# A decoder layer on one core: ten gathered rows moved in front of the up-projection, and the small products of token mixing spread over four row groups

## The chip, the cores and the metric

The kernel runs on one core of a Trainium2 chip. The metric is the device time of one execution in microseconds (us). Engines are named as in the profile: PE (matrix products; PEld its weight loads), DVE (VectorE), ACT (ScalarE), POOL (GpSimd, which issues the indirect DMAs), SP (the queue that issues most other DMAs).

## What is computed

One decoder layer on 512 tokens of width 1024: token mixing (an mLSTM with four heads beside sliding-window attention), cross-attention into 256 memory tokens, and PEER, a layer of 128 x 128 single-neuron experts of which each token uses 8 heads x 16.

```python
h = h + concat([hm, ha]) @ w_out          # token mixing: mLSTM heads, attention heads
h = h + memory_cross_attention(rmsnorm(h, g_cross), rmsnorm(mem, g_mem), ...)
h = h + peer_ffn(rmsnorm(h, g_ffn), ...)
# peer_ffn: u = expert_down[eidx]; a = gelu(einsum("thkd,td->thk", u, x)); coef = g * a
#           out = einsum("thkd,thk->td", expert_up[eidx], coef)
return rmsnorm(h, g_final)
```

Inside the mLSTM the decay of one head is `d = exp(log_d - m_t)` with `log_d` the sum of a row that depends on the query, a column that depends on the key, and the causal mask.

## The kernel before, in words

The 512 tokens are four blocks of 128. Products in fp32 precision are made of three products of rounded parts (hi x hi, lo x hi, hi x lo); a product of plain fp32 operands is two passes on PE.

**Token mixing** (`front`). The input projection is done as GEMMs (`gemm_tm`, `gemm_fm`). For the mLSTM decays, `ra` is a tile of four partitions (one for each head) by 512 tokens. For each head, L218 multiplies it by a selector `sel` of four rows, which copies the head's row to all 128 partitions of the PSUM tile `ab`; L219 adds the causal mask `cmask`; ACT takes the exponential in four pieces (L222, tile `dt`). L230 makes the scores `st` of two heads from operands of 64 partitions each, L233 (DVE) multiplies scores and decays. L238 does for `wi` (two tiles `wb`) what L218 does for `ra`. PE fills the time between with the last input GEMM (`acc_f`, for `aq`). Then a list of letters, `MIX`, sets PE's order by hand: s is a step of window attention of a block (`sp` scores, `tp_p` transposes, `o_att`), m a step of the mLSTM, n the transposes `tp_hm` of its output, x a half of the output GEMM (`acc_o`), w the load of a weight.

**PEER** treats the blocks in two ways. Blocks 1 to 3 run over all 128 x 128 experts densely: for each of 128 "down tiles" (`Down`, 24 products `acc_d`) and 128 "up tiles" (`up_tile` and `up_mm`, 18 products `acc_u` of 512 columns). Their gates are scattered into the DRAM tensors `wd` by POOL (L672) or written there from `stg` by ACT's queue (L731), and read back as `wt` (L855). Block 0 is done sparsely by `gather`: 128 indirect DMAs fetch one row of `expert_down` per token each (L749, 128 x 1024 fp32), DVE takes the dot product of each with the token (L755, `dots`); then 128 more fetch rows of `expert_up`, and DVE adds each with its coefficient to `gacc` (L765). One call of `step(ga, 1)` does one row. Eight buffers `rows` hold the fetched rows, so a fetch waits for DVE to be done with the row eight before.

The rows of block 0 are laid out among the dense work: twelve in the last block of `gating` (at the steps in `GQ`), the other 244 in the loop over up tiles, by the weights `WST` and `WTL` and up to tile `GST` = 122 (the list `due`, L1165 to L1168). Between the two lie the `LEAD` = 7 down tiles that PE does before the first up tile. After the loop `finish` adds `gacc` and the PSUM sums to the residual `hb` (L907), normalises (L913) and writes out. A scheduler in the build then fixes each engine's order; on the chip each engine runs its list strictly in that order.

Of the kernel before, what the change touches and what calls it, by code (L numbers as in the profile page):

```python
# [48 lines left out]


GQ = range(9, 32, 2)
GST = 122
WST, WTL = 3, 5


# [2 lines left out]

MIX = ("w0 s0 s0 n0 n1 s1 m2 s1 x0 m2 s0 w1 x1 s0 m3 x0 s2 s1 s2 s1 s3 s1 s3 n2 x1 x2 s2 n3 s2 x3 s2 s3 x2 s3 s3 x3")


CROSS = "m0 o0 K1 K0 V0 V1 n0 q0 s0 s1 q1 s2 p0 s3 p1 p2 p3"
# [15 lines left out]
def front(c):  # L80
# [66 lines left out]
    A.activation(u, gf, AF.Abs)  # L147
    A.activation(u, u, AF.Exp, scale=-1.0)
    V.tensor_scalar(w1, u, 1.0, None, op0=ALU.add)
    ra = fp.tile([4, NB, P], F32, name="ra")  # L150
    raf = ra.rearrange("p b t -> p (b t)")
    V.scalar_tensor_tensor(raf, w1, -1.0, u, op0=ALU.add, op1=ALU.subtract)
    A.activation(w1, w1, AF.Ln)
    V.tensor_tensor(w1, w1, raf, op=ALU.subtract)
# [4 lines left out]
    V.memset(rs[:, :, 0:1], 0.0)  # L159
    V.tensor_tensor_scan(u, rs.rearrange("p b t -> p (b t)"), gf, 0.0, op0=ALU.mult, op1=ALU.add)  # L160
    V.tensor_tensor(raf, u, m, op=ALU.subtract)
    V.tensor_tensor(gi, gi, u, op=ALU.subtract)
    mp = fp.tile([4, NB], F32, name="mp")
    al = fp.tile([4, NB], F32, name="al")
# [3 lines left out]
    rows = f1.tile([P, S], F32, name="rows")  # L168
    V.memset(rows, 0.0)
    V.tensor_copy(rows[0:4], gi)  # L170
    wi = fp.tile([4, NB, P], F32, name="wi")
    for b in range(NB):
        t = slice(b * P, (b + 1) * P)
        A.activation(rows[32:36, t], gi[:, t], AF.Exp, bias=al[:, b:b + 1])
        A.activation(wi[:, b], ra[:, b], AF.Exp, bias=mp[:, b:b + 1])
    A.activation(rows[64:68], m, AF.Exp, scale=-1.0)
    cols = fp.tile([P, NB, 96], F32, name="cols")
    for b in range(NB):
        tp = ps.tile([P, 512], F32, tag="a", name="tp_r")
# [30 lines left out]
    gemm_tm(c, [a["w_in_m"][2, hf] for hf in range(2)], evac_mo)  # L210


    pt = []
    for pr in range(2):
        dts = []
        for h in (2 * pr, 2 * pr + 1):
            ab = ps.tile([P, 512], F32, tag="d", name="ab")
            T.matmul(ab, c.sel[:, h], raf, start=True, stop=False)  # L218
            T.matmul(ab, c.identb, c.cmask, start=False, stop=True)  # L219
            dt = c.np_.tile([P, D], F32, tag="xs", bufs=4, name="dt")[:, :S]  # L220
            for b in range(NB):
                A.activation(dt[:, b * P:(b + 1) * P], ab[:, b * P:(b + 1) * P], AF.Exp, bias=cols[:, b, h:h + 1])  # L222
            dts.append(dt)

        sts = [ps.tile([P, 512], F32, tag="a", name="st") for _ in range(2)]
        for b in range(NB):
            t = slice(b * P, (b + 1) * P)
            for hh in range(2):
                r = slice(64 * hh, 64 * hh + 64)
                T.matmul(sts[hh][:, t], qk[r, 2 + pr, t], qk[r, pr, t], start=True, stop=True)  # L230
        for hh in range(2):
            pth = fp.tile([P, S], F32, name=f"pt{2 * pr + hh}")
            V.tensor_tensor(pth, sts[hh], dts[hh], op=ALU.mult)  # L233
            pt.append(pth)
    dec = fp.tile([P, 2, NB], F32, name="dec")
    for pr in range(2):
        wb = ps.tile([P, 512], F32, tag="d", name="wb")
        T.matmul(wb, c.selp[:, pr], wi.rearrange("p b t -> p (b t)"), start=True, stop=True)  # L238
        V.tensor_copy(dec[:, pr], wb.rearrange("p (b t) -> p b t", b=NB)[:, :, P - 1])
        V.tensor_tensor(qk[:, pr], wb, qk[:, pr], op=ALU.mult)  # L240
    def make_kw(b):
# [818 lines left out]
def front_consts(c):  # L1060
    nc, a, cp = c.nc, c.a, c.fp
    V, G = nc.vector, nc.gpsimd
    c.gmh = cp.tile([P, 512], F32, name="gmh")
    c.sinks = cp.tile([P, 8], F32, name="sinks")
    with c.tc.issue_after(c.x_dma.ins):
        nc.sync.dma_start(c.gmh, a["prow"][0, 5120:5632].partition_broadcast(P))
        nc.sync.dma_start(c.sinks, a["prow"][0, 5632:5640].partition_broadcast(P))

    c.cmask = cp.tile([P, 512], BF16, name="cmask")
    z = c.np_.tile([P, D], F32, tag="xs", bufs=4, name="zmask")  # L1070
    V.memset(z[:, :512], 0.0)
    cm = c.np_.tile([P, D], F32, tag="xs", bufs=4, name="cm32")
    G.affine_select(cm[:, :512], z[:, :512], [[0, NB], [1, P]], ALU.is_ge, NEG, base=0, channel_multiplier=-1)
    V.tensor_copy(c.cmask, cm[:, :512])
    c.band = cp.tile([P, 256], F32, name="band")

    G.affine_select(c.band[:, 0:P], z[:, 0:P], [[1, P]], ALU.is_gt, NEG, base=0, channel_multiplier=-1)
    G.affine_select(c.band[:, P:256], z[:, 0:P], [[-1, P]], ALU.is_ge, NEG, base=0, channel_multiplier=1)

    c.sel = cp.tile([4, 4, P], F32, name="sel")  # L1080
    o = c.np_.tile([P, D], F32, tag="xs", bufs=4, name="ones4")[0:4, 0:512].rearrange("p (h q) -> p h q", h=4)
    V.memset(o, 1.0)
    G.affine_select(c.sel, o, [[1, 4], [0, P]], ALU.is_equal, 0.0, base=0, channel_multiplier=-1)
    c.selp = cp.tile([4, 2, P], F32, name="selp")
    G.affine_select(c.selp, o[:, 0:2], [[2, 2], [1, 2], [0, 64]], ALU.is_equal, 0.0, base=0, channel_multiplier=-1)


def body(tc, a, out, dbg=None):
# [3 lines left out]
    with ExitStack() as st:  # L1092
# [57 lines left out]
        with pool("gather", side="right") as c.gp:  # L1150
# [4 lines left out]
            c.up = st.enter_context(pool("up"))  # L1155
            assert len(gel) == SP

            ahead(LEAD)
            c.rowid = c.gp.tile([P, P], I32, name="rowid")
            with tc.issue_after(c.dl.ins):  # L1160
                nc.vector.tensor_copy(c.rowid, c.eidx)
            pst_ = [c.ps.tile([P, 512], F32, tag=t, name="acc_u") for t in "bbbbaa"]
            acc = [[pst_[2 * b], pst_[2 * b + 1]] for b in range(ND)]
            last, mms = [], []
            g0 = len(GQ)  # L1165
            due = [WST * u + WTL * made_by(u) for u in range(-1, GST)]
            rows = [(2 * P - g0) * (d - due[0]) // (due[-1] - due[0]) for d in due]
            rows += [rows[-1]] * (NK - GST)  # L1168
# [102 lines left out]
```

## Time and profile before

| | |
|---|---|
| median of 3 runs | 1662.37 us (1662.21 to 1662.63) |
| the profiled execution's own time | 1659.86 us |
| its span | 1658.1 us |
| PE / DVE / ACT / POOL busy, share of span | 97% / 74% / 44% / 36% |
| chain that ended last, by engine | PE 89%, DVE 5%, DMA 3%, ACT 2%, issue 1% |
| PE's granted clock over the span | 0.989 |

The profile is one execution. The profiled execution lies 2.5 us under the median, and its span 1.8 us under its own time. A view by windows gives the busy time of each engine in a stretch; a timeline gives the instructions in order with the idle time before each in square brackets and what ended it.

### The profile page before, as it was taken

To read this page: it belongs to the slowest core of one execution; us is meant where nothing else is said; L and a number is where in the kernel's file an instruction comes from. 1 tells how busy PE (TensorE), PEld (TensorE's weight loads), DVE (VectorE), ACT (ScalarE), POOL (GpSimd) and SP (SyncE) were. 2 spreads that over 40 slices of the span, in tenths; PEclk is the share of its full clock that TensorE was granted. 3 is DMA by queue.
4 is the path that set the end of the run, shared out by engine and by line. 5 is a ranking of instruction groups with operands and counts; after the bars stand their busy time and mean duration, and the time that the engine had idled before them with its cause. 6 is when DMAs were issued, how large, how long until landed. Compare 5 with 4: busy or idle time off the path is not lost.

```text
span 1658.1 us, 23086 instructions
## 1 busy us (share of the span) xinstructions
PE 1610.6 (97%) x8387; PEld 1412.3 (85%) x8388; DVE 1233.9 (74%) x2698; ACT 722.7 (44%) x1215; POOL 600.4 (36%) x427
## 2 busy tenths in 40 slices
PE   9999999999999999999999999999999999999992
PEld 5766698878999999999999888888888888888881
DVE  5546564564878888777884888788878788888898
ACT  5435544443544444577764333333333333333331
POOL 2000000000027787878103445344434344444443
PEclk9999999999999999999999999999999999999996
DMA  6236234232254435668969999999989899998886
GB/s 213 77 127 245 73 136 157 76 153 106 96 188 124 115 80 132 204 178 226 347 203 366 409 384 352 336 342 339 351 339 328 347 342 334 336 344 316 323 316 242
DMA packets 151122, 402.17 MB, mean 243 GB/s; under 512 B 28368, under 2 KB 62304, under 8 KB 138848
## 3 DMA queue, kind: packets, MB, share of 16 engines
q1 hardware_dynamic: 58208, 240.04, 39.0%
q0 software_dynamic: 55360, 134.32, 24.5%
q10 hardware_dynamic: 37440, 26.35, 5.1%
q8 instruction: 66, 1.08, 0.3%
q14 instruction: 48, 0.39, 0.1%
HBM read 357.07 MB, written 43.58 MB: 242 GB/s over the span
## 4 chain that ended last, share of the span: by engine, by line
PE 89%; DVE 5%; DMA 3%; ACT 2%; issue 1%; POOL 0%; DVEq 0%; POOLq 0%; ACTq 0%
PE acc_u L894 10%; PE acc_u L895 10%; PE acc_u L896 10%; PE acc_d L823 10%; PE acc_d L822 10%; PE acc_d L821 10%; PE acc_f L995 4%; PE acc_f L997 4%; PE acc_f L996 4%; PE w L727 3%; DMA wd<-stg 3%; PE acc_t L1010 2%; PE acc_t L1009 2%; PE acc_t L1008 2%; DVE gacc L765 1%
## 5 line engine op out<-in xcount | busy, mean ns | idle before, releaser
L821 PE MATMUL acc_d<-xhi,dh 128*128 128x384 f32 x1024 | 349.2, 341 | 0.0
L823 PE MATMUL acc_d<-xhi,dl 128*128 128x384 f32 x1024 | 344.7, 337 | 1.4 <-DVE dl L810 1.3
L822 PE MATMUL acc_d<-xlo,dh 128*128 128x384 f32 x1024 | 343.1, 335 | 0.0
L896 PE MATMUL acc_u<-uh,cl 128*128 128x512 f32 x762 | 297.7, 391 | 0.0
L895 PE MATMUL acc_u<-ul,ch 128*128 128x512 f32 x762 | 297.6, 391 | 0.0
L672 POOL DMA_INDIRECT wd<-gg,ei x128 | 231.2, 1806 | 147.4 <-DVE ei L666 84.8
L894 PE MATMUL acc_u<-uh,ch 128*128 128x512 f32 x762 | 263.5, 389 | 0.0
L749 POOL DMA_INDIRECT rows<-in_up_dram,rowid x128 | 175.7, 1372 | 214.3 <-DVE gacc L765 187.4
L749 POOL DMA_INDIRECT rows<-in_down_r_dram,rowid x116 | 155.4, 1339 | 264.2 <-DVE dots L755 177.8
L810 DVE TENSOR_TENSOR dl<-draw,dh 128x1024 fp32r<-128x1024 f32 x128 | 156.2, 1221 | 97.0 <-ACT dh L772 92.3
L772 ACT CAST dh<-draw 128x1024 fp32r<-128x1024 f32 x128 | 134.1, 1049 | 198.9 <-PE acc_d L822 184.6
L882 ACT CAST ch<-cf 128x384 fp32r<-128x384 f32 x127 | 65.2, 514 | 354.6 <-issue 332.5
L821 PEld LDWEIGHTS acc_d<-xhi,dh 128*128 128x128 f32 x1024 | 192.6, 188 | 3.8
L823 PEld LDWEIGHTS acc_d<-xhi,dl 128*128 128x128 f32 x1024 | 192.2, 188 | 4.0 <-DVE dl L810 2.6
L822 PEld LDWEIGHTS acc_d<-xlo,dh 128*128 128x128 f32 x1024 | 192.5, 188 | 3.5
L896 PEld LDWEIGHTS acc_u<-uh,cl 128*128 128x128 f32 x762 | 143.0, 188 | 29.6
L895 PEld LDWEIGHTS acc_u<-ul,ch 128*128 128x128 f32 x762 | 143.0, 188 | 28.8
L894 PEld LDWEIGHTS acc_u<-uh,ch 128*128 128x128 f32 x762 | 142.8, 188 | 27.7
L873 DVE TENSOR_TENSOR ul<-uraw,uh 128x1024 fp32r<-128x1024 f32 x127 | 155.0, 1221 | 15.1 <-ACT uh L772 14.7
L765 DVE SCALAR_TENSOR_TENSOR gacc<-rows,coef,gacc 128x1024 f32<-128x1024 f32 x127 | 162.6, 1280 | 1.1
L755 DVE CUSTOM_DVE_ANT_0 rows<-rows,xn 128x1024 f32<-128x1024 f32 x128 | 154.0, 1219 | 0.0
L883 DVE TENSOR_TENSOR cl<-cf,ch 128x384 fp32r<-128x384 f32 x127 | 70.8, 558 | 85.8 <-ACT ch L882 85.2
(338 smaller groups left out, 2644.6 us busy)
## 6 DMA issues: line engine op xcount, KB each, us to landing
draw<-in_down_t_dram SPq DMA_DIRECT2D x64, 1024.0 KB, 6.5
uraw<-in_up_dram SPq DMA_DIRECT2D x64, 1024.0 KB, 9.1
wt<-wd SPq DMA_DIRECT2D x96, 256.0 KB, 8.8
wd<-stg ACTq DMA_DIRECT2D x8, 2048.0 KB, 16.0
gd<-gsp SPq DMA_DIRECT2D x18, 768.0 KB, 4.0
gsr<-gd SPq DMA_DIRECT2D x18, 768.0 KB, 9.8
wd<-zero ACTq DMA_DIRECT2D x1, 8192.0 KB, 27.3
raw<-in_w_pq_dram SPq DMA_DIRECT2D x8, 1024.0 KB, 4.9
```

Source lines behind the costliest of these rows:

```text
L672: i = G.indirect_dma_start(out=out, out_offset=bass.IndirectOffsetOnAxis(ap=ei[:, h, k:k + 1], axis=0), in_=c.gg[:, NG, hh, k:k + 1], in_o ...
L749: G.indirect_dma_start(out=r, out_offset=None, in_=src, in_offset=bass.IndirectOffsetOnAxis(ap=c.rowid[:, j:j + 1], axis=0))
L755: V.tensor_tensor_reduce(r, r, c.xn0, 1.0, 0.0, op0=ALU.mult, op1=ALU.add, accum_out=dots[:, j:j + 1])
L765: V.scalar_tensor_tensor(c.gacc, r, coef[:, j:j + 1], c.gacc, op0=ALU.mult, op1=ALU.add)
L810: c.dl = nc.vector.tensor_tensor(self.lo, raw, f32(self.hi), op=ALU.subtract)
L821: T.matmul(acc[:, :TD], self.hi[:, ks], c.xhi[:, k, NG * P:], start=(k == 0), stop=False)
L822: T.matmul(acc[:, :TD], self.hi[:, ks], c.xlo[:, k, NG * P:], start=False, stop=False)
L823: T.matmul(acc[:, :TD], self.lo[:, ks], c.xhi[:, k, NG * P:], start=False, stop=(k == KT - 1))
L873: V.tensor_tensor(lo, raw, f32(hi), op=ALU.subtract)
L894: T.matmul(acc[b][n], ch[:, t], hi[:, d], start=st, stop=False)
L895: T.matmul(acc[b][n], ch[:, t], lo[:, d], start=False, stop=False)
L896: c.mm = T.matmul(acc[b][n], cl[:, t], hi[:, d], start=False, stop=sp)
```

## The change

On the side of PEER: `GLD` = 10 rows of `gather` are stepped among the seven lead tiles, each bound behind a down tile's `dl` on DVE, and the loop's share is cut to match (256 - 22 rows up to tile 120 in place of 256 - 12 up to tile 122). On the side of token mixing: `ra`, `sel`, `wi` and `selp` are copied to further groups of partitions (at 32, 64 and 96, four rows each), the four products of the heads stand one behind the other, each on another group, and then the four masks; the two products for `wb` use groups 0 and 32. `MIX` is written in another order (n2 and n3 earlier).

```diff
--- before.py
+++ after.py
@@ -49,7 +49,8 @@
 
 GQ = range(9, 32, 2)
-GST = 122
+GLD = 10
+GST = 120
 WST, WTL = 3, 5
 
@@ -58,7 +59,7 @@
 
 
-MIX = ("w0 s0 s0 n0 n1 s1 m2 s1 x0 m2 s0 w1 x1 s0 m3 x0 s2 s1 s2 s1 s3 s1 s3 n2 x1 x2 s2 n3 s2 x3 s2 s3 x2 s3 s3 x3")
+MIX = ("w0 s0 s0 n0 n1 s1 m2 s1 x0 m2 s0 w1 x1 s0 m3 x0 s2 s1 s2 s1 s3 n2 s1 n3 s3 x2 x1 s2 s2 s2 x3 s3 x2 s3 s3 x3")
 
 CROSS = "m0 o0 K1 K0 V0 V1 n0 q0 s0 s1 q1 s2 p0 s3 p1 p2 p3"
@@ -147,8 +148,10 @@
     A.activation(u, gf, AF.Abs)
     A.activation(u, u, AF.Exp, scale=-1.0)
     V.tensor_scalar(w1, u, 1.0, None, op0=ALU.add)
-    ra = fp.tile([4, NB, P], F32, name="ra")
-    raf = ra.rearrange("p b t -> p (b t)")
+
+    ra4 = fp.tile([P, NB, P], F32, name="ra")
+    raf4 = ra4.rearrange("p b t -> p (b t)")
+    ra, raf = ra4[0:4], raf4[0:4]
     V.scalar_tensor_tensor(raf, w1, -1.0, u, op0=ALU.add, op1=ALU.subtract)
     A.activation(w1, w1, AF.Ln)
     V.tensor_tensor(w1, w1, raf, op=ALU.subtract)
@@ -159,6 +162,9 @@
     V.memset(rs[:, :, 0:1], 0.0)
     V.tensor_tensor_scan(u, rs.rearrange("p b t -> p (b t)"), gf, 0.0, op0=ALU.mult, op1=ALU.add)
     V.tensor_tensor(raf, u, m, op=ALU.subtract)
+    A.copy(raf4[32:36], raf)
+    V.tensor_copy(raf4[64:68], raf)
+    A.copy(raf4[96:100], raf)
     V.tensor_tensor(gi, gi, u, op=ALU.subtract)
     mp = fp.tile([4, NB], F32, name="mp")
     al = fp.tile([4, NB], F32, name="al")
@@ -168,12 +174,14 @@
     rows = f1.tile([P, S], F32, name="rows")
     V.memset(rows, 0.0)
     V.tensor_copy(rows[0:4], gi)
-    wi = fp.tile([4, NB, P], F32, name="wi")
+    wi4 = fp.tile([36, NB, P], F32, name="wi")
+    wi = wi4[0:4]
     for b in range(NB):
         t = slice(b * P, (b + 1) * P)
         A.activation(rows[32:36, t], gi[:, t], AF.Exp, bias=al[:, b:b + 1])
         A.activation(wi[:, b], ra[:, b], AF.Exp, bias=mp[:, b:b + 1])
     A.activation(rows[64:68], m, AF.Exp, scale=-1.0)
+    V.tensor_copy(wi4[32:36], wi)
     cols = fp.tile([P, NB, 96], F32, name="cols")
     for b in range(NB):
         tp = ps.tile([P, 512], F32, tag="a", name="tp_r")
@@ -210,17 +218,20 @@
     gemm_tm(c, [a["w_in_m"][2, hf] for hf in range(2)], evac_mo)
 
-    pt = []
+    pt, dts = [], []
+
+    abs_ = [ps.tile([P, 512], F32, tag=t_, name="ab") for t_ in "ddaa"]
+    for h in range(4):
+        r = slice(32 * h, 32 * h + 4)
+        T.matmul(abs_[h], c.sel[r, h], raf4[r], start=True, stop=False)
+    for h in range(4):
+        T.matmul(abs_[h], c.identb, c.cmask, start=False, stop=True)
+    for h in range(4):
+        dt = c.np_.tile([P, D], F32, tag="xs", bufs=4, name="dt")[:, :S]
+        for b in range(NB):
+            A.activation(dt[:, b * P:(b + 1) * P], abs_[h][:, b * P:(b + 1) * P], AF.Exp, bias=cols[:, b, h:h + 1])
+        dts.append(dt)
     for pr in range(2):
-        dts = []
-        for h in (2 * pr, 2 * pr + 1):
-            ab = ps.tile([P, 512], F32, tag="d", name="ab")
-            T.matmul(ab, c.sel[:, h], raf, start=True, stop=False)
-            T.matmul(ab, c.identb, c.cmask, start=False, stop=True)
-            dt = c.np_.tile([P, D], F32, tag="xs", bufs=4, name="dt")[:, :S]
-            for b in range(NB):
-                A.activation(dt[:, b * P:(b + 1) * P], ab[:, b * P:(b + 1) * P], AF.Exp, bias=cols[:, b, h:h + 1])
-            dts.append(dt)
 
         sts = [ps.tile([P, 512], F32, tag="a", name="st") for _ in range(2)]
         for b in range(NB):
@@ -230,12 +241,14 @@
                 T.matmul(sts[hh][:, t], qk[r, 2 + pr, t], qk[r, pr, t], start=True, stop=True)
         for hh in range(2):
             pth = fp.tile([P, S], F32, name=f"pt{2 * pr + hh}")
-            V.tensor_tensor(pth, sts[hh], dts[hh], op=ALU.mult)
+            V.tensor_tensor(pth, sts[hh], dts[2 * pr + hh], op=ALU.mult)
             pt.append(pth)
     dec = fp.tile([P, 2, NB], F32, name="dec")
-    for pr in range(2):
-        wb = ps.tile([P, 512], F32, tag="d", name="wb")
-        T.matmul(wb, c.selp[:, pr], wi.rearrange("p b t -> p (b t)"), start=True, stop=True)
+    wbs = [ps.tile([P, 512], F32, tag="d", name="wb") for _ in range(2)]
+    for pr in (1, 0):
+        r = slice(32 * pr, 32 * pr + 4)
+        T.matmul(wbs[pr], c.selp[r, pr], wi4[r].rearrange("p b t -> p (b t)"), start=True, stop=True)
+    for pr, wb in enumerate(wbs):
         V.tensor_copy(dec[:, pr], wb.rearrange("p (b t) -> p b t", b=NB)[:, :, P - 1])
         V.tensor_tensor(qk[:, pr], wb, qk[:, pr], op=ALU.mult)
     def make_kw(b):
@@ -1077,12 +1090,15 @@
     G.affine_select(c.band[:, 0:P], z[:, 0:P], [[1, P]], ALU.is_gt, NEG, base=0, channel_multiplier=-1)
     G.affine_select(c.band[:, P:256], z[:, 0:P], [[-1, P]], ALU.is_ge, NEG, base=0, channel_multiplier=1)
 
-    c.sel = cp.tile([4, 4, P], F32, name="sel")
+    c.sel = cp.tile([P, 4, P], F32, name="sel")
     o = c.np_.tile([P, D], F32, tag="xs", bufs=4, name="ones4")[0:4, 0:512].rearrange("p (h q) -> p h q", h=4)
     V.memset(o, 1.0)
-    G.affine_select(c.sel, o, [[1, 4], [0, P]], ALU.is_equal, 0.0, base=0, channel_multiplier=-1)
-    c.selp = cp.tile([4, 2, P], F32, name="selp")
-    G.affine_select(c.selp, o[:, 0:2], [[2, 2], [1, 2], [0, 64]], ALU.is_equal, 0.0, base=0, channel_multiplier=-1)
+    G.affine_select(c.sel[0:4], o, [[1, 4], [0, P]], ALU.is_equal, 0.0, base=0, channel_multiplier=-1)
+    for h in range(1, 4):
+        V.tensor_copy(c.sel[32 * h:32 * h + 4, h], c.sel[0:4, h])
+    c.selp = cp.tile([36, 2, P], F32, name="selp")
+    G.affine_select(c.selp[0:4], o[:, 0:2], [[2, 2], [1, 2], [0, 64]], ALU.is_equal, 0.0, base=0, channel_multiplier=-1)
+    V.tensor_copy(c.selp[32:36, 1], c.selp[0:4, 1])
 
 def body(tc, a, out, dbg=None):
@@ -1155,14 +1171,17 @@
             c.up = st.enter_context(pool("up"))
             assert len(gel) == SP
 
-            ahead(LEAD)
+            for n in range(LEAD):
+                ahead(1)
+                with tc.issue_after(c.dl.ins):
+                    step(ga, GLD * (n + 1) // LEAD - GLD * n // LEAD)
             c.rowid = c.gp.tile([P, P], I32, name="rowid")
             with tc.issue_after(c.dl.ins):
                 nc.vector.tensor_copy(c.rowid, c.eidx)
             pst_ = [c.ps.tile([P, 512], F32, tag=t, name="acc_u") for t in "bbbbaa"]
             acc = [[pst_[2 * b], pst_[2 * b + 1]] for b in range(ND)]
             last, mms = [], []
-            g0 = len(GQ)
+            g0 = len(GQ) + GLD
             due = [WST * u + WTL * made_by(u) for u in range(-1, GST)]
             rows = [(2 * P - g0) * (d - due[0]) // (due[-1] - due[0]) for d in due]
             rows += [rows[-1]] * (NK - GST)
```

The built program's order shows three places where the prediction rests. First PE in `front`, behind the last product of the gate GEMM (`ab` decays, `st` scores, `acc_f` the GEMM that fills in). Before:

```order
L218 MATMUL ab<-ra,sel 128x512
L219 LDWEIGHTS identb
L219 MATMUL ab<-cmask,identb 128x512
L218 MATMUL ab<-ra,sel 128x512
L219 LDWEIGHTS identb
L219 MATMUL ab<-cmask,identb 128x512
L230 MATMUL st<-qk 128x128 x8
```

Now:

```order
L226 MATMUL ab<-ra,sel 128x512 x4
L228 LDWEIGHTS identb
L228 MATMUL ab<-cmask,identb 128x512
L228 LDWEIGHTS identb
L228 MATMUL ab<-cmask,identb 128x512
L228 LDWEIGHTS identb
L228 MATMUL ab<-cmask,identb 128x512
L228 LDWEIGHTS identb
L228 MATMUL ab<-cmask,identb 128x512
L1008 MATMUL acc_f_958<-xhi,whi 128x512
```

Before, the other two heads follow later among the `acc_f`; now all four stand together, and the scores come later. The two `wb` products keep two `acc_f` products between them.

Second DVE at the lead tiles (`dl` is a down tile's low part, the two `ISA` rows are one row of `dots`, `cf`, `cl` and `ul` the parts of the first up tiles). Before:

```order
L755 ISA rows,dots<-rows,xn_2910 128x1024
L755 ISA dots 128x1
L810 TENSOR_TENSOR dl<-draw,dh 128x1024 x4
L880 TENSOR_TENSOR cf<-gel,wt 128x384 x2
L810 TENSOR_TENSOR dl<-draw,dh 128x1024
L883 TENSOR_TENSOR cl<-cf,ch 128x384 x2
L880 TENSOR_TENSOR cf<-gel,wt 128x384 x2
L873 TENSOR_TENSOR ul<-uraw,uh 128x1024 x2
```

Now, from the fourth of those `dl`:

```order
L823 TENSOR_TENSOR dl<-draw,dh 128x1024
L768 ISA rows,dots<-rows,xn_2918 128x1024
L768 ISA dots 128x1
L768 ISA rows,dots<-rows,xn_2918 128x1024
L768 ISA dots 128x1
L823 TENSOR_TENSOR dl<-draw,dh 128x1024
L768 ISA rows,dots<-rows,xn_2918 128x1024
L768 ISA dots 128x1
L893 TENSOR_TENSOR cf<-gel,wt 128x384 x2
L886 TENSOR_TENSOR ul<-uraw,uh 128x1024 x2
L896 TENSOR_TENSOR cl<-cf,ch 128x384 x2
```

One or two rows of `dots` stand behind each `dl`, and the first `cf` now stands behind one more `dl` and its row. One of the ten rows stands still earlier, in front of the last steps of `gating`.

Third DVE at the end (`xlo` holds the last up tile's low part, `hb` the residual). Before:

```order
L873 TENSOR_TENSOR xlo<-uraw,xlo 128x1024
L765 SCALAR_TENSOR_TENSOR gacc<-rows,coef,gacc 128x1024 x16
L907 TENSOR_TENSOR hb<-hb,gacc 128x512 x2
L907 TENSOR_TENSOR hb<-hb,acc_u 128x512 x2
L909 TENSOR_TENSOR frst<-fss 128x1
```

Now:

```order
L886 TENSOR_TENSOR xlo<-uraw,xlo 128x1024
L778 SCALAR_TENSOR_TENSOR gacc<-rows,coef,gacc 128x1024 x7
L920 TENSOR_TENSOR hb<-hb,gacc 128x512 x2
L920 TENSOR_TENSOR hb<-hb,acc_u 128x512 x4
L922 TENSOR_TENSOR frst<-fss 128x1
```

Behind the last instruction that PE needs from DVE stood sixteen rows of `gacc`, and now stand seven; the some 120 DVE instructions ahead of it are the same as before.

## Rows read from the trace of the kernel before

**Rows 1.** Windows: busy us of each engine (count), granted clock, DMA share, GB/s.

```profile
1620.00:1640.00 20.00, 5.59 (x25) 4.31 (x23) 19.50 (x16) 0.00 (x0) 10.42 (x9) 0.69 0.88 321
```

**Rows 2.** Timeline of DVE at the end: start, us, engine, line, operation.

```profile
1615.90 1.27 DVE L765 SCALAR_TENSOR_TENSOR gacc<-rows,coef,gacc 128x1024 f32<-128x1024 f32 x1
...
1620.56 21.10 DVE L765 SCALAR_TENSOR_TENSOR gacc<-rows,coef,gacc 128x1024 f32<-128x1024 f32 x16
1641.69 1.29 DVE L907 TENSOR_TENSOR hb<-hb,gacc 128x512 f32<-128x512 f32 x2
```

**Rows 3.** Timelines of PE and POOL at the end, and DMA issues (median us to landing).

```profile
1625.20 0.39 PE L896 MATMUL acc_u<-xlo 128*128 128x512 f32 x1
...
1617.44 1.68 POOL L749 DMA_INDIRECT rows<-in_up_dram,rowid  x1 [0.66 <-DVE gacc L765]
...
rows<-in_up_dram,rowid POOLq DMA_INDIRECT x128, 6.7
```

**Rows 4.** Groups of DVE, 860 to 890 us (busy, mean ns; idle before), and its timeline.

```profile
L810 DVE TENSOR_TENSOR dl<-draw,dh 128x1024 fp32r<-128x1024 f32 x6 | 7.3, 1224 | 15.3 <-ACT dh L772 15.3
L755 DVE CUSTOM_DVE_ANT_0 rows<-rows,xn 128x1024 f32<-128x1024 f32 x1 | 1.2, 1224 | 0.0
...
884.28 1.03 DVE L880 TENSOR_TENSOR cf<-gel,wt 128x384 f32<-128x384 f32 x2 [2.54 <-DMA wt<-wd]
```

**Rows 5.** Timelines of SP's queue, ACT and PE around the first up tile.

```profile
869.93 12.06 SPq L855 DMA_DIRECT2D wt<-wd  x3
...
887.47 2.01 ACT L772 CAST uh<-uraw 128x1024 fp32r<-128x1024 f32 x2 [1.61 <-DMA uraw<-in_up_dram]
...
890.42 1.08 PE L894 MATMUL acc_u<-uh,ch 128*128 128x512 f32 x4
```

**Rows 6.** The chain's writes of the gates, a window, and DMA issues and a queue, 770 to 900 us.

```profile
782.84 26.19 DMA wd<-stg
...
865.84 15.82 DMA wd<-stg
...
870.00:880.00 10.00, 10.00 (x59) 10.00 (x58) 1.70 (x2) 2.50 (x4) 0.00 (x0) 1.00 1.01 334
...
rows<-in_down_r_dram,eidx POOLq DMA_INDIRECT x12, 13.3
...
q10 hardware_dynamic: 23448, 11.96, 31.3%
```

**Rows 7.** The chain on PE: start, us, line, passes; and PE's timeline.

```profile
101.81 1.05 PE ab L218 x2
...
115.02 1.10 PE st L230 x16
...
416.55 0.89 PE s L567 x8
...
103.12 1.12 PE L218 MATMUL ab<-ra,sel 4*128 4x512 f32 x2 [0.25 <-issue]
```

**Rows 8.** Windows in token mixing.

```profile
101.70:105.40 3.70, 3.45 (x22) 1.69 (x22) 1.58 (x1) 3.49 (x3) 0.00 (x0) 1.00 0.00 0
105.40:108.90 3.50, 3.50 (x14) 2.61 (x11) 2.70 (x4) 2.37 (x9) 0.00 (x0) 0.51 0.38 114
...
146.40:149.80 3.40, 3.40 (x16) 2.37 (x16) 3.40 (x17) 0.59 (x1) 0.00 (x0) 0.50 1.04 380
```

**Rows 9.** What PE waited for, 95 to 207 us: us in total, times, longest.

```profile
PE acc_o L1010 <- DVE xlo L930: 2.1, 2, 1.1
...
PE tp_p L350 <- DVE pT L355: 0.5, 1, 0.5
PE sp L318 <- ACT aq L371: 0.4, 1, 0.4
...
PE sp L318 <- DVE mx L323: 0.3, 1, 0.3
```

**Rows 10.** A DVE copy of four partitions in token mixing: duration min/median/max, start.

```profile
L170 DVE COPY rows<-gi x1: 416/416/416, 66.0 to 66.0; 4x512 f32<-4x512 f32 x1
```

## The prediction

> **What bounds the kernel now.** I read the view of groups by engine first, then the chain that ended last: PE is busy 97% of the span and 89% of the chain, so a change pays only where PE stands still, works slower than it could, or is already done. There are three such places, and the change touches all three.
>
> The end. In the window from 1620 us PE works 5.59 of 20 us, DVE 19.50 [rows 1]. DVE's timeline says with what: behind its last operand for PE come sixteen `gacc` in 21.10 us, and only then `hb` [rows 2]. PE's last product starts at 1625.20 and takes 0.39 [rows 3]. So from 1625.6 to 1641.7 the kernel waits for DVE alone.
>
> The lead tiles. From 860 to 890 us DVE waits 15.3 us for `dh`, in front of six `dl`; a row of `dots` costs 1224 ns there, and the first `cf` has itself waited 2.54 for `wt` [rows 4]. The reader sees here a DVE with room, and a chain that runs elsewhere: SP's queue has stood 12.06 us for `wt`, `uh` was cast at 887.47, `acc_u` begins at 890.42 [rows 5]. What SP waits for is a write of gates, 15.82 us long, after one of 26.19; both stand on the chain [rows 6].
>
> Token mixing. PE makes each head's `ab` in two passes in 1.05 us [rows 7], then runs a stretch at granted clock 0.51 [rows 8], and waits a little for DVE and ACT [rows 9].
>
> The base is the profiled execution, 1659.86 us; its span stands 1.8 below that, and the median of the runs 2.5 above. I make the sum against 1659.9 and add 2.5. Less than 0.2%, 3.3 us, cannot be told from no change here.
>
> **The end: -11.9, and +0.6 back.** One `gacc` costs 21.10 / 16 = 1.319 us [rows 2]. Seven stay behind the last `xlo`, so nine go: 9 x 1.319 = 11.9. In front of it stand 244 - 16 = 228 rows before and 234 - 7 = 227 now, in a phase where PE hides them, so nothing is paid there. Two things could bound the end instead. PE: `hb` would now start near 1641.7 - 11.9 = 1629.8, still 4 us behind PE's end. The last fetched row: with eight buffers it waits for the `gacc` eight before, the one at 1615.90; POOL issued at 1617.44 for 1.68, and a row lands a median 6.7 us after its issue [rows 2, 3]. That makes 1625.8, and it is needed at 1620.56 + 6 x 1.319 = 1628.5. DVE still bounds, with 2.7 us to spare. The four `hb` now stand in another order, sums of `gacc` first; one half (1.29 / 2 = 0.65 [rows 2]) may come later: +0.6, from 0 to 1.2.
>
> **The lead: +2.0.** Ten rows at 1.224, plus some 0.085 for the small instruction behind each, are 13.1 us of DVE. They fit the 15.3 that it waits for `dh` [rows 4], so DVE's work I cost at nothing; if that cover were gone, the next `dl` would be late, and PE behind it. The first `cf` now stands behind a sixth `dl` and its row: 885.2 + 2.6 = 887.8 at the earliest, one more microsecond for `ch`, and PE wants it at 890.42. It fits.
>
> What I charge is transfers. One row stands ahead of the last steps of `gating`: the last gate write starts 1.3 us later. And rows that DVE finishes while that write runs free buffers, so that POOL fetches two or three more rows, 512 KB each, into a DMA that is busy 1.01 of the window at 334 GB/s [rows 6]: 0.5 MB / 334 to 400 GB/s is 1.3 to 1.6 us each, about 2.9 for two. Queued behind that write are SP's `wt`, and behind `wt` the `uraw` that ACT casts to `uh`. Its slack: the first `uh` was ready at 888.5, PE began at 890.42, so 1.9. 1.3 + 2.9 - 1.9 = 2.3; since not all of a fetch need fall into the write, I take +2.0. Bounds: 0, and 26.19 - 15.82 - 1.9 = 8.5, if the write takes as long as the longest shown. I stay near the low end because the fetches' bytes are counted and 26.19 belongs to another place.
>
> **Mixing, the products: -3.1.** Four `ab` one behind another cost 4 x 1.05 = 4.2 us. Whether products on separate four-row groups overlap, no row shows for four. For two it is shown: sixteen `st` passes, whose heads lie on two groups of 64 rows, took 1.10 us or 69 ns each, while eight passes `s` of all rows took 0.89, or 111 ns [rows 7]. Two groups thus give 1.6. Between nothing saved and a perfect four (4.2 / 4 = 1.05, so 3.15) I take 2.9, since starts were close to free in the pair; and one of the issue gaps of 0.25 behind a change of groups goes too [rows 7]: -3.1, from 0 to -3.4. The pair for `wb` keeps two `acc_f` between its parts: 0.
>
> [...]
>
> **Mixing, the clock: -1.7.** [...]
>
> **Mixing, the order: -1.8.** `acc_o` waited 2.1 us for `xlo` [rows 9]; with n2 and n3 earlier the transposes and the rounding are done long ahead. 0.7 of waits at `sp` [rows 9] may be filled by the mLSTM steps that now stand there. Against that, an `o_att` now stands directly behind its transposes and waits for the copy `pT`, nearest the 0.5 of [rows 9], twice at most: +1.0. Sum -1.8, from 0 to -2.8. The new copies of `ra` and `wi` cost some 0.42 to 0.63 us each (one of four partitions took 416 ns, at 66 us [rows 10]), a good 25 us ahead of the first `ab` at 101.8, beside PE's GEMM: 0, or +1.0 without that cover.
>
> What mixing gains, -6.6, reaches the end, since PE is all but full from there on. **Sum:** -11.9 + 0.6 + 2.0 - 6.6 = -15.9. That is 1644.0 for the profiled execution, 1646.5 for the median.
>
> **The rivals.**
> *The fetches pace the end.* `rows` land later than 6.7 us after issue, because nine fewer rows leave the last fetch only 2.7 us to spare and the DMA share there is 0.88 [rows 1]. Half the gain at the end goes: +6.0, 1652.4. Against it: the median is over 128 fetches under the same load.
> [...]
> *The lead stalls.* The write of gates takes 26.19 again: 8.5 in place of 2.0, 1653.0. [...]
> *More of it.* Both slow stretches go, every wait goes, the lead costs nothing: -11.9 - 3.4 - 3.4 - 2.8 = -21.5, 1640.9.
> *Slower.* All ten fetches stand in front of the last gate write. At 13.3 us from issue to landing [rows 6] and eight at a time that is 10 / 8 x 13.3 = 16.6 us, and 10.4 more for the long write: 27.0 + 1.3 - 1.9 = 26.4 us in which PE has no up tile to do. The gains without the lead are 17.9, so 8.5 is lost: 1670.9. It becomes slower from a stall of 17.9 + 3.3 = 21.2. Against it: a fetch can follow only when DVE has used the row eight before, and most of the ten are fetched before the write begins.
>
> **How the numbers follow.** Chances: forecast 0.60, with a range of its own from 1642 (second stretch gone, the lead free: -3.7, and 0.6 at the end) to 1651 (clock, order and copies give nothing: +1.7 + 1.8 + 1.0); fetches at the end 0.12; mixing gives nothing 0.13; the lead 0.07; more 0.05; slower 0.03. The range from 1641.0 to 1653.5 takes in all but the slower case, half of the case with more, and the upper halves of the three around 1653: about 0.2 outside. All cases but one are gains above 3.3; between them and the slower one I leave 0.02 for no change. Faster 0.95, same 0.02, slower 0.03.
>
> **What would show it.** Seven `gacc` behind the last `xlo` in 9.2 us, without a wait for `rows`, and `hb` some 4 us behind PE's end. All four `ab` within 1.4 us. No window at 0.5 right behind them, and no wait of `acc_o` for `xlo`. At the lead, a first `acc_u` that PE waits for by 2 us, ended by `uraw` or `wt`. The forecast is wrong if PE's wait there is over 8 us, if DVE waits for `rows` at the end, or if the four `ab` take 4 us.

## The result, and the profile after

The changed kernel takes 1653.64 us (median of 5, 1651.02 to 1655.91) against 1662.21 of the kernel before, measured beside it: ratio 0.995, interval 0.9935 to 0.9964. It is faster by 8.6 us, about half of the 15.9 forecast, and lies 0.1 us above the range. Measured twice more, it had ratios of 0.996 (0.9947 to 0.9972) and 0.9947 (0.9932 to 0.9961).

Five marks of PE cut the span into stretches, in us (first and last records of the tiles named; profiled executions, which are 6.6 apart):

| stretch | before | changed | difference | forecast |
|---|---|---|---|---|
| token mixing: first `ab` to end of last `acc_o` | 109.34 | 109.85 | +0.5 | -6.6 |
| from there to the last product `w` of gating | 654.10 | 657.31 | +3.2 | +1.3 (in the lead's +2.0) |
| lead: last `w` to first `acc_u` | 25.24 | 25.89 | +0.7 | rest of the +2.0 |
| first to last `acc_u` | 735.17 | 735.30 | +0.1 | 0 |
| PE's end to the end of the span | 32.5 | 21.4 | -11.1 | -11.3 |

The end came as forecast. DVE's timeline of the changed kernel (start, us, engine, line, operation):

```profile
1623.92 1.22 DVE L886 TENSOR_TENSOR xlo<-uraw,xlo 128x1024 fp32r<-128x1024 f32 x1
1625.05 9.20 DVE L778 SCALAR_TENSOR_TENSOR gacc<-rows,coef,gacc 128x1024 f32<-128x1024 f32 x7
1634.29 1.29 DVE L920 TENSOR_TENSOR hb<-hb,gacc 128x512 f32<-128x512 f32 x2
1635.50 2.47 DVE L920 TENSOR_TENSOR hb<-hb,acc_u 128x512 f32<-128x512 f32 x4
```

Seven `gacc` in 9.20 where sixteen took 21.10 [rows 2], none with a wait for `rows`; `hb` starts 4.2 us behind PE's last product (1630.1), so DVE still sets the end.

The lead, in the chain that ended last, and DVE's timeline:

```profile
869.54 17.34 DMA wd<-stg
887.26 4.97 DMA uraw<-in_up_dram
892.31 2.00 ACT uh L785 x2
```

```profile
862.92 1.22 DVE L768 CUSTOM_DVE_ANT_0 rows<-rows,xn 128x1024 f32<-128x1024 f32 x1
864.06 0.08 DVE L768 DVE_READ_ACCUMULATOR2_ANT dots<- 128x1 f32 x1
864.06 1.34 DVE L739 TENSOR_SCALAR oh<-iota,I2T,gT 128x128 f32<-128x128 f32 x4
```

The gate write takes 17.34 where it took 15.82 [rows 6], and one row of 1.22 stands ahead of the last `oh`. In the chain, `uraw` now stands where `wt` stood. The sign named for the lead, a wait of PE for 2 us at the first `acc_u`, did not come: it waits 0.18 there. Ahead of that it waits 1.00 for `gsp` (ACT's part of a down tile) and 0.65 for a `dl`, whose `dh` came late because ACT had waited 2.53 for the transfer `draw`.

In token mixing the products did what the change says. PE's timeline: eight passes for four heads in 1.14 us, where one head's two passes took 1.05 on the chain [rows 7]:

```profile
101.73 1.14 PE L226 MATMUL ab<-ra,sel 4*128 4x512 f32 x8
102.80 1.04 PE L228 MATMUL ab<-cmask,identb 128*128 128x512 bf16 x4
```

And yet the stage ends no sooner. In the lines that follow, `num` are the products of the mLSTM from which DVE makes a block's output `hm`, `ds` is the update of its state, `mx` the largest score of window attention, and `aq` its queries, which the `acc_f` make. The waits of PE from 95 to 212 us (us in total, times, longest), and three windows (PE, PE load, DVE, ACT, POOL busy, granted clock, DMA share, GB/s):

```profile
PE acc_o L1021 <- DVE mx L336: 3.2, 1, 3.2
PE ds L298 <- DVE hm L289: 1.7, 1, 1.7
PE tp_hm L312 <- DVE hm L310: 1.5, 1, 1.5
PE o_att L373 <- ACT pT L366: 1.1, 1, 1.1
```

```profile
140.87:147.69 6.82, 5.32 (x23) 3.51 (x23) 5.02 (x21) 5.56 (x25) 1.01 (x1) 0.50 1.04 374
178.41:185.24 6.83, 6.00 (x14) 4.77 (x15) 2.89 (x13) 4.94 (x19) 0.00 (x0) 0.50 0.00 0
816.71:820.12 3.41, 3.41 (x14) 3.41 (x14) 2.41 (x6) 0.83 (x2) 1.14 (x1) 0.50 1.00 361
```

The wait of `acc_o` for `xlo` [rows 9] is gone, but the four waits shown, 7.5 us in all, stand in the stage. The stretch at half clock behind the `ab` [rows 8] is gone too in this profile; one twice as long begins between the two waits for `hm`, and another during the long one for `mx`. In all 13.7 us at 0.50 in mixing, where there were 6.8. The third window lies in gating, outside the forecast.

### The profile page after: what moved, and what is told of

It is laid out like the page before. It is cut to its first block, busy times and chain, and to the rows that moved or that the text cites. A ratio compares the mean times of both kernels' runs of the same rounds, so it can differ in the third digit from the quotient of the medians.

```text
span 1651.5 us, 23090 instructions
## 1 busy us (share of the span) xinstructions
PE 1609.7 (97%) x8388; PEld 1415.1 (86%) x8388; DVE 1235.1 (75%) x2704; ACT 723.6 (44%) x1217; POOL 591.1 (36%) x427
## 4 chain that ended last, share of the span: by engine, by line
PE 89%; DVE 4%; DMA 3%; ACT 2%; issue 1%; POOL 0%; DVEq 0%; SPq 0%; POOLq 0%; ACTq 0%
PE acc_u L907 10%; PE acc_u L908 10%; PE acc_u L909 10%; PE acc_d L836 10%; PE acc_d L834 10%; PE acc_d L835 10%; PE acc_f L1008 4%; PE acc_f L1009 4%; PE acc_f L1010 4%; PE w L740 3%; DMA wd<-stg 3%; PE acc_t L1023 2%; PE acc_t L1022 2%; PE acc_t L1021 2%; DVE gacc L778 1%
## 5 line engine op out<-in xcount | busy, mean ns | idle before, releaser
L762 POOL DMA_INDIRECT rows<-in_up_dram,rowid x128 | 169.4, 1323 | 236.8 <-DVE gacc L778 208.9
L762 POOL DMA_INDIRECT rows<-in_down_r_dram,rowid x106 | 142.6, 1346 | 199.1 <-DVE dots L768 158.4
```

The costliest lines, as they stand in the source:

```text
L762: G.indirect_dma_start(out=r, out_offset=None, in_=src, in_offset=bass.IndirectOffsetOnAxis(ap=c.rowid[:, j:j + 1], axis=0))
```

## The experiments

Ratios are to the kernel before, measured beside each version, with 95% intervals. "Mixing" is the first row of the table above, "slow" the time at half clock (granted 0.50 or 0.51) within it, both of one profiled execution. Diffs show the lines that matter; `...` stands for lines left out.

**One part of the change at a time.** The products on row groups alone, with the old list of steps and no rows in the lead:

```diff
-GLD = 10
-GST = 120
+GST = 122
...
-MIX = ("w0 s0 s0 n0 n1 s1 m2 s1 x0 m2 s0 w1 x1 s0 m3 x0 s2 s1 s2 s1 s3 n2 s1 n3 s3 x2 x1 s2 s2 s2 x3 s3 x2 s3 s3 x3")
+MIX = ("w0 s0 s0 n0 n1 s1 m2 s1 x0 m2 s0 w1 x1 s0 m3 x0 s2 s1 s2 s1 s3 s1 s3 n2 x1 x2 s2 n3 s2 x3 s2 s3 x2 s3 s3 x3")
...
```

> Only the token-mixing products on four row groups; the list of steps and the gathered rows as in the kernel before. Theory O (the new order of steps costs what the products give, by a 3.21 us wait of PE for mx and by two slow-clock stretches twice as long): the products alone give 3 to 5 us, 1657 to 1659, last acc_o of mixing 3 to 5 us earlier than in the kernel before (211.1). Rival D (mixing is paced by the DVE and ACT chain of hm and mx, so PE only waits more, whatever the order): within 1.5 us of before, 1661 to 1663.5, with the gain of the products seen again as waits for hm and mx.

1662.26 against 1661.11 us, ratio 1.0011 (1.0001 to 1.002): nothing gained, outside Theory O's forecast and inside Rival D's. Mixing 110.90, slow 13.7, and PE waits 3.3 us for `hm`.

The new list alone (one line of the kernel before, `MIX`):

> Only the new list of steps. Theory O: slower by 2 to 5 us (1664 to 1667), with the 3.21 us wait for mx and slow stretches of 6.8 us behind the waits. Rival D: within 1.5 us of before. My forecast said 1.8 us faster.

1660.17, ratio 0.9994 (0.9985 to 1.0003). It costs nothing, so Theory O falls: mixing 109.08, and no wait for `hm`.

The ten rows alone:

```diff
+GLD = 10
-GST = 122
+GST = 120
...
-ahead(LEAD)
+for n in range(LEAD):
+    ahead(1)
+    with tc.issue_after(c.dl.ins):
+        step(ga, GLD * (n + 1) // LEAD - GLD * n // LEAD)
...
-g0 = len(GQ)
+g0 = len(GQ) + GLD
```

> Only the ten rows at the lead tiles; token mixing as before. Theory: 11.1 us gained behind PE's end, 1.9 lost between the last gates and the first up tile (1.2 by the row ahead of the last oh, 0.7 by the longer write): -9.2, 1653. Rival G (the rows also cost the 2.2 us that the changed kernel loses at 814 us in gating, 0.6 of wait and 1.6 of slow clock): -7.0, 1655. If all of the changed kernel's gain is here, this kernel is within 1.5 us of the changed one (1653.6).

1652.61, ratio 0.9952 (0.9939 to 0.9965): 8.5 faster. All that the change gained is here. (Of its two numbers only `GLD` counts: built with `GST` 120 or 122, the kernel before has the same order on DVE.)

The changed kernel with the old list:

> The changed kernel with the old list of steps: products and rows, not the order. Theory O: 3 to 5 us faster than the changed kernel, 1649 to 1651. Rival D: the same as the changed kernel within 1.5 us, 1652 to 1655.

1651.37, ratio 0.9944 (0.9931 to 0.9957), between the two forecasts; mixing was 112.05 in its profile, slow 17.1. What the list does beside the products these runs don't separate.

**Is it the groups, or where the products stand?** Two heads at a time on two groups, the first `st` right behind them:

```diff
-abs_ = [ps.tile([P, 512], F32, tag=t_, name="ab") for t_ in "ddaa"]
-for h in range(4):
-    r = slice(32 * h, 32 * h + 4)
-    T.matmul(abs_[h], c.sel[r, h], raf4[r], start=True, stop=False)
...
+for pr in range(2):
+    abs_ = [ps.tile([P, 512], F32, tag="d", name="ab") for _ in range(2)]
+    for hh in range(2):
+        r = slice(64 * pr + 32 * hh, 64 * pr + 32 * hh + 4)
+        T.matmul(abs_[hh], c.sel[r, 2 * pr + hh], raf4[r], start=True, stop=False)
...
```

The masks, the exponentials and the `st` of a pair follow in the same loop.

> The changed kernel, but the decay products two heads at a time (two groups, PSUM tiles of tag d as before), so that the first st stands right behind the first pair again. Theory M (with all four heads at once, two of the PSUM tiles that st needs are held until ACT has taken the exponentials; st, num and hm come 3 us or more later against acc_f, the filler is used up, PE waits for hm and its clock falls for longer): PE's 1.65 and 1.50 us waits for hm shrink below 0.6, slow stretches in mixing 6.8 us in all in place of 13.7; 1.5 to 4 us faster than the changed kernel of this call. Rival H (products on several groups lower the clock wherever they stand): slow stretches stay at 13 us, time within 1 us of the changed kernel.

1651.56, ratio 0.9935 (0.9923 to 0.9947), beside 1653.99 of the changed kernel:

> The changed kernel once more, beside the next three on the same chip. Both theories: 1652 to 1655.

Mixing 107.49, slow 3.4, no wait for `hm`, as Theory M had it; Rival H, that products on several groups lower the clock wherever they stand, falls. No products on groups, but rows and list:

> Ten rows and the new list of steps, products as before. By the sum of the two parts run alone (-8.5 and -0.9): 9.4 faster than before, and by Theory M 1 to 2 us faster than the changed kernel, since the products are what costs. Rival (the parts do not add, the new order needs the products): within 0.5 us of the changed kernel or slower.

1650.11, ratio 0.9932 (0.992 to 0.9945). The gain is 11.0 us, where the two parts alone add up to 9.4, which lies inside the interval; and the changed kernel is 3.9 slower than itself without its products, where 1 to 2 were forecast. The converse, the four together but one after another, with every engine's order that of the changed kernel:

```diff
-r = slice(32 * h, 32 * h + 4)
+r = slice(0, 4)
 T.matmul(abs_[h], c.sel[r, h], raf4[r], start=True, stop=False)
```

> The changed kernel with the four decay products together as there, but all on the first group of partitions, so that they run one after another; every engine's order is the changed kernel's. Theory M (the place of the four products costs, the groups themselves give about 3 us of PE): ab takes 4.2 us or more in place of 1.1, and PE waits for hm and slow stretches stay as in the changed kernel (over 2.5 us and over 10 us); 1655 to 1658, slower than the changed kernel by 1.5 to 4. Rival H (groups lower the clock): slow stretches fall to 7 us or less, time 1651 to 1654.

1657.93, ratio 0.9979 (0.9968 to 0.9989), beside a repetition of rows and list:

> The ten rows with the new list of steps and the products as before, once more, beside the next three: 1650 to 1651.

1650.76. PE's timeline of the serial one, and its waits:

```profile
102.08 4.04 PE L226 MATMUL ab<-ra,sel 4*128 4x512 f32 x8
```

```profile
PE acc_o L1021 <- DVE mx L336: 3.2, 1, 3.2
PE tp_hm L312 <- DVE hm L310: 1.7, 1, 1.7
PE ds L298 <- DVE hm L289: 1.7, 1, 1.7
```

4.04 against 1.14 us for the same eight passes: the groups give 2.9, and with all four on one group the kernel gains 3.3 us on the kernel before, where the changed kernel gained 7.1 to 8.7. So the groups work (Theory M), and putting the four together costs 7.2 us against rows and list alone; the fast products pay back a part. The copies of `ra` and `wi` are in these 7.2, but they are in the kernel with the pairs too, and that one lies 1.5 us from rows and list. Waits and slow time (13.7) are those of the changed kernel.

**What the place does.** The 96 `acc_f` are PE's filler: work that it can do while it waits for other engines. In the built order, eleven of them stand between the second block's `num` and its `ds` before the change, and none after it: all have been used earlier, while the first `st` came 8 us later (112.57 in place of 104.49). Two edits tell the two sides apart. The first binds the last twelve `acc_f` behind that `num` (`hold` is its last product); the second lets the first two heads take the PSUM tiles of tag `a`, which `st` wants next:

```diff
...
+if hold is not None and hf and j == 3:
+    with c.tc.issue_after(hold.ins):
+        mm3_fm(c, acc[j], w, j, hf, S)
...
```

```diff
-for t_ in "ddaa"
+for t_ in "aadd"
```

> The changed kernel, with the last twelve acc_f products bound behind the num products of the second block, so that they stand where PE waited 1.65 us for hm; nothing else on PE moves but four sp. Theory F (the filler is used up too early): waits for hm below 1 us in place of 3.2, slow stretches in mixing 7 us or less in place of 13.7, 2 to 4 us faster than the changed kernel, 1650 to 1652. Rival T (the chain of st, pt, num and hm is late in itself): PE waits as long, only elsewhere (for aq or mx at sp); within 1 us of the changed kernel.

> The changed kernel, but the first two heads' products take the PSUM tiles of tag a and the last two those of tag d, so that st's tiles are free after eight exponentials and not sixteen; in the built order thirteen acc_f then stand between ds and the next num. Theory F and Theory T both: st one to two us earlier, waits for hm smaller. F: they go by the acc_f that stand there, below 1 us, 2 to 4 us faster than the changed kernel. T: by the one to two us of st alone, 0 to 2 us faster.

> The changed kernel once more, for the two ahead of it: 1653 to 1655, slow stretches of 13.7 us and waits for hm of 3.2 us in mixing.

The kernel of the first edit took 1651.1 us (0.9921 to 0.9948 as a ratio), the second 1651.7 (0.992 to 0.9946) and the changed kernel 1652.59 (0.9932 to 0.9961): too close to call by time. This profile of the changed kernel shows mixing 112.95, slow 17.1 and 2.7 us of waits for `hm`, not the 13.7 and 3.2 expected. By its profile the first edit takes away most of the waits for `hm` and the slow stretch behind them, but brings one for `aq`, which those `acc_f` make:

```profile
PE acc_o L1021 <- DVE mx L336: 3.2, 1, 3.2
PE sp L331 <- ACT aq L384: 1.9, 1, 1.9
PE o_att L373 <- ACT pT L366: 1.0, 1, 1.0
PE ds L298 <- DVE hm L289: 0.8, 1, 0.8
```

Slow time is 10.2, where Theory F said 7 or less, mixing takes 110.60, and PE stands idle for 8.8 us of it, against 8.5 in the first profile of the changed kernel: by itself this edit moved the waits, as Rival T had it. With the second alone, `st` came 7.2 us behind the first `ab` in place of 10.8, but 3.8 us of waits at `ds` and `tp_hm` stayed, as did 13.7 us of slow clock; PE's idle time was 9.4. My count there was wrong: thirteen `acc_f` stand ahead of that `num`, where they cover nothing. Both together, beside rows and list once more:

> The changed kernel with the tiles of tag a first and with twelve acc_f held behind the num products of the second block. Theory F: the waits for hm and the slow stretch behind them go, the products' own 3 to 4 us stay: 1648 to 1650, 1 to 2 us under the kernel without the products. Rival (token mixing is set by the chain through mx and aq on DVE and ACT, so what PE saves comes back as another wait): within 1 us of the kernel without the products.

> The ten rows with the new list of steps and the products as before, a third time: 1650 to 1651.

1644.32 us (1642.53 to 1645.33), ratio 0.99 (0.9882 to 0.9918), against 1650.54 (0.9921 to 0.9955): the fastest version, and 6.2 us under the kernel without the products, where Theory F said 1 to 2. The window over token mixing in the changed kernel and in this one:

```profile
101.70:212.00 110.30, 101.80 (x526) 71.58 (x526) 61.50 (x209) 57.34 (x181) 5.16 (x6) 0.94 0.36 129
```

```profile
101.70:212.00 110.30, 104.39 (x564) 73.62 (x564) 64.55 (x215) 60.72 (x187) 5.17 (x6) 1.00 0.39 139
```

No slow stretch; mixing takes 102.04, 7.3 less than in the kernel before. PE's timeline shows the place:

```profile
135.31 0.40 PE L1010 MATMUL acc_f<-xhi,wlo 128*128 128x512 f32 x1
135.64 0.49 PE L331 MATMUL sp<-kT,aq 64*128 64x128 f32 x4
136.06 0.66 PE L298 MATMUL ds<-vx,kw 128*64 128x129 f32 x8
138.22 0.49 PE L331 MATMUL sp<-kT,aq 64*128 64x128 f32 x4 [1.50 <-ACT aq L384]
```

`ds` comes without a wait, since twelve `acc_f` ran while DVE made `hm`. The later `acc_o` waits 1.5 us where it waited 3.2 for `mx`. PE's idle time in mixing is 5.9 us, against 8.5 in the changed kernel and 6.1 before, so against the kernel before hardly any of the 7.3 comes from waits. By my estimate 3.1 come from the `ab` (4.2 to 1.14) and 3.4 from the missing 6.8 us at half clock, and 1.0 from something that neither edit was meant for: with the tiles of tag `a` first, the two `wb` products stand side by side, in this kernel and in that of the second edit alone,

```profile
110.00 1.13 PE L250 MATMUL wb<-wi,selp 4*128 4x512 f32 x4
```

four passes in 1.13 us, where in the kernel before and in the changed one each of the two products took 1.12.

**How many rows.** Fourteen, five (the same line), and ten with none ahead of the last `oh`, each from the kernel with rows and list:

```diff
-GLD = 10
+GLD = 14
```

```diff
-step(ga, GLD * (n + 1) // LEAD - GLD * n // LEAD)
+step(ga, GLD * n // (LEAD - 1) - GLD * max(n - 1, 0) // (LEAD - 1))
```

> The kernel before it with fourteen rows at the lead tiles: four gacc behind the last xlo in place of seven. Theory (end bound by DVE, lead with room): 3 x 1.319 = 4.0 less at the end, 0 to 1.5 more at the lead: 2.5 to 4 faster than that kernel. Rival (the lead's transfers are at their limit: four more fetches of 512 KB at 334 GB/s, 1.6 us each, stand in front of the gates): 4 or more lost at the lead, no gain or slower.

1656.74, ratio 0.9977 (0.9967 to 0.9988): 6.6 slower than ten, the rival's side. The end gave its 4.0 (four `gacc` in 5.24 us), but the lead grew from 26.6 to 33.5 and the up phase by 4.0. Its waits of PE from 860 to 930 us and a window:

```profile
PE acc_d L822 <- ACT dh L773: 6.0, 3, 4.1
PE acc_u L895 <- ACT ch L883: 2.6, 1, 2.6
```

```profile
914.51:921.34 6.83, 5.06 (x12) 4.10 (x13) 5.08 (x8) 3.74 (x5) 2.14 (x2) 0.50 1.01 403
```

The DMA share is 1.01 at 403 GB/s, `draw` comes late (at 915 us ACT has waited 8.1 for it), PE waits for `dh`, and within the wait of 4.1, which ends at 916.28, its granted clock is 0.50.

> Five rows in place of ten. Eleven gacc stay behind the last xlo: 4 x 1.319 = 5.3 more at the end. Theory (ten rows cost 2.8 us around the lead, five half of it or less): 1.4 to 2.8 back, net 2.5 to 3.9 slower than ten, 1652.5 to 1654. Rival (the lead's cost is that of one row ahead and not of transfers): 5.3 slower less nothing, 1655.5.

1653.86, ratio 0.9952 (0.9939 to 0.9964): 3.1 slower than ten, inside the forecast. Five rows lost 5.0 at the end (26.4 in place of 21.4) and won 1.9 back; the two profiles show 0.8 of it, in the lead and ahead of it.

> The ten rows spread over the last six of the seven lead tiles, so that none stands ahead of the last steps of gating. Theory: the last gate write starts 1.3 us earlier; eight gacc in place of seven behind the last xlo give 1.3 back: the same as the kernel before it within 1 us, the time from the last product w to the first acc_u not longer than there (26.6 us). Rival (the fetches bunched into fewer tiles stand in front of the gates): 2 us or more slower.

1650.5, ratio 0.9935 (0.9922 to 0.9948), the same as with one ahead, as forecast: the lead took 26.3 us, the end 1.3 more, and the gate write 19.07.

## Why the prediction was wrong

**The end: right.** -11.9 for nine `gacc` was 21.10 - 9.20 = 11.9; with the finish it came to -11.1 where -11.3 was forecast. Not one fetch paced it.

**The lead: right in kind and nearly in size.** The row ahead of the last `oh` takes 1.2, and the lead grew by 0.7 with a write longer by 1.5: 1.9, for a forecast of 2.0. With the rows alone the stretch ahead of the lead grew by 1.6 and the lead by 1.3; the twelve other profiles with these ten rows lost 0.6 to 1.7 in the lead itself, so 2 to 3 us in all is the better figure. The write is longer with rows in the lead: 15.82 without, 16.49 with five rows, 17.2 to 17.8 with ten, 19.07 with ten in six tiles. By what means the fetches lengthen it no run shows, and 26 us it never took there. Some 2 us more were lost at 814 us in gating (0.6 more of a wait of PE for `oh`, and the stretch at half clock above). Three of the profiles have this stretch, all with the rows and with products on groups, while eleven with the same ten rows have not; why is open.

**Mixing, the products: right.** -3.1 was forecast; 4.04 less 1.14 is 2.9, and with the order kept the kernel gained 4 to 5 us more with the groups than without. The eight passes took 4.04 / 1.14 = 3.5 times as long on one group as on four. The gap of 0.25 called issue [rows 7], which the forecast counted as one more gain, is most likely work: it stands in the place of the first of the four mask products, and the trace has records of the other three alone (L219, 0.39 each).

**Mixing, the clock and the order: these steps failed.** The -1.7 is half of the 3.50 us at granted clock 0.51 [rows 8]; that this stretch would go was my estimate, and no run shows that term, the +1.7 of the range or the -3.4 of "More of it" by itself. What the first profile showed in its place: that one was not seen, but the time at half clock doubled, from 6.8 to 13.7. That half of such time is lost is an estimate too, from the granted clock; in the kernel before, one `acc_f` starts 0.43 us after another in that stretch, and 0.23 after another behind it:

```profile
106.26 0.63 PE L996 MATMUL acc_f<-xlo,whi 128*128 128x512 f32 x1
106.69 0.63 PE L997 MATMUL acc_f<-xhi,wlo 128*128 128x512 f32 x1
...
109.31 0.39 PE L995 MATMUL acc_f<-xhi,whi 128*128 128x512 f32 x1
109.54 0.40 PE L996 MATMUL acc_f<-xlo,whi 128*128 128x512 f32 x1
```

For 2.3 us of the 13.7 PE stood idle anyway (it was busy for 5.32 of 6.82 and 6.00 of 6.83), so by that estimate half of the other 11.3, less half of 6.8, is the loss: +2.2. "0.7 of waits at `sp` may be filled", "Sum -1.8": the `xlo` waits went as forecast, and with them one that the sum had left out:

```profile
PE acc_o L1008 <- ACT xhi L929: 1.5, 1, 1.5
```

But other waits came: against the 6.1 us of gaps on PE's timeline from 102 to 212 us before stand 8.5 now, +2.4. Even alone the new list did less than the -1.8: gaps of 5.3, so -0.8, with 1.5 for `den` at the `acc_o` in place of the 3.6 for `xlo` and `xhi`, and a time that is not clear of noise (-0.9). Together clock and waits made +4.6 where -3.5 stood; with 3.1 gained by the products that is +1.5, where +0.5 was measured and -6.6 forecast.

What I had priced at nothing is a fact that I had shown myself in the order: four heads together, "and the scores come later". I looked only at what the four products cost PE, and not at what then runs out: `acc_f`, the filler of the whole stage, was used up ahead of the waits that it used to cover. That the place of the four costs, and not the groups, is shown: 7.2 us by the serial kernel, and with the pairs the waits for `hm` are gone. That the cost comes by way of the filler and of the late `st` is shown only for the two together: twelve `acc_f` put back alone left 8.8 us of gaps, `st` earlier alone 9.4, neither telling by time, and both together 5.9, with a gain of 16.2 us on the kernel before, where the changed kernel gained 7.1 to 8.7. How much each of the two is worth stays open.

These 16.2 us are near the 15.9 forecast for the change, and mixing gains 7.3 for 6.6. Part of that is luck, for in the profiled execution the terms are not those forecast: waits -0.2 for -1.8, the clock -3.4 for -1.7, and `wb` -1.0 for 0.

**The rivals.** The measured time is near 1662.4 - 9.3 = 1653.1, what the end and the lead give (-11.9 + 0.6 + 2.0) when mixing gives nothing, to which the forecast left 0.13. Mixing did give nothing, but not for want of the products, which ran side by side (1.14 us against 4.04): clock and waits moved, and their gain was spent there. The slower case and the lead's long stall did not come; the point from which the lead turns lies between ten and fourteen rows.

## What to carry to other kernels

When a change makes PE's work shorter or moves it forward, list the work that fills its waits and count how much of it stands behind each wait afterwards: with the products on groups this stage gained where PE no longer waited for `hm` (107.49 and 102.04 us against 109.34), and not where it did (109.85 to 112.95 in the profiles above). A faster product and its place are two edits, and each is worth a run of its own; here the one gave 3 to 5 us and the other took 7, by the serial kernel, and only with twelve products put back and the PSUM tiles freed earlier did the stage gain what was forecast (7.3 for 6.6). The rows moved to an idle engine were paid in transfers: ten fitted (8.5 us gained by them alone), and four more cost more than they gave (6.6 us slower).

## What was not expected of the hardware

The place of the slow stretches changes between executions of the same program. The kernel with rows and list had one, from 145.13 to 148.55, in one execution, and two in another, each beside an `st`:

```profile
145.13:148.55 3.42, 3.42 (x16) 2.38 (x18) 3.42 (x17) 0.53 (x1) 0.00 (x0) 0.50 1.04 380
```

```profile
104.62:108.03 3.41, 3.41 (x20) 2.65 (x20) 3.20 (x3) 3.38 (x10) 0.00 (x0) 0.50 0.09 24
114.86:118.27 3.41, 3.41 (x20) 2.52 (x19) 0.34 (x1) 1.14 (x4) 0.00 (x0) 0.50 0.00 0
```

PE's records fill all of these three windows (3.42 of 3.42 us, 3.41 of 3.41 twice): a full PE at granted clock 0.50. Mixing took 107.5 and 110.2 us. The changed kernel differs as much: 13.7 us at half clock in two profiles, from 140.9 and 178.4 or close to it, and 17.1 in the third, from 112.7, 143.5 and 191.2. So one stretch in one profile is no term of a sum by itself. What held in every profile is the total: 10.2 us or more in the eight with the four products together and the filler used up or only part of the way back, 6.8 or less in the ten others, and none in the version with both edits. Each profile is one execution. The granted clock recorded with that version's five executions was 0.995 in three, 0.992 in two: since 0.50 is granted in such a stretch, the difference, 0.003 x 1643 x 2, is an estimated 10 us more at half clock somewhere in these two. They took 1645.2 and 1645.3 us, still 2.5 under the fastest of rows and list beside them (1647.82), so the gain is not a matter of the clock alone.
